# One z pair moved out of the direct stretch, sums of y moved into the merge, and first loads by three queues, in a Mamba/short-conv/SwiGLU block

## The chip, the cores and the metric

The kernel runs on one core of one Trainium2 chip. Its time is the device time of one execution in microseconds (us), the median of several runs; lower is better. A core has five engines that work side by side, each on a queue of its own in the order of the program: PE (TensorE, matrix products; its weight loads are listed as PEld), DVE (VectorE, elementwise), ACT (ScalarE, activations and scaled copies), POOL (GpSimd) and SP (SyncE). Transfers between the chip's memory (HBM) and the on-chip memory (SBUF) are started by an instruction on SP's, ACT's or POOL's queue and then run on 16 DMA engines. An instruction that waits for its data holds up whatever stands behind it in its own queue. PSUM is the small memory of eight banks into which PE writes.

## The reference

One encoder block on x of 1024 rows by 1024 columns, all in float32:

```
h  = rmsnorm(x)
z, xbc, dt, s_b, s_c, s_x, g_a, g_b = split(h @ w_in)
xbc = silu(causal conv of 4 taps(xbc) + bias);  xs, B, C = split(xbc)
y   = chunked state-space scan(xs, softplus(dt + bias), -exp(a_log), B, C) + d_skip * xs
y   = y * silu(z);  y = rmsnorm of y in 4 groups of 512 columns * ssd_norm_w
a   = y @ w_ssd_proj
b   = (s_b * causal conv of 3 taps(s_c * s_x)) @ w_sconv_proj
h1  = x + (sigmoid(g_a) * a + sigmoid(g_b) * b) @ w_o
h2  = h1 + (silu(n @ w_gate) * (n @ w_up)) @ w_down,   n = rmsnorm(h1)
out = rmsnorm(h2) * final_norm_w
```

## The kernel before

Everything is kept transposed: features on the 128 partitions, the 1024 time steps along the row. A tile is 128 features by 1024 steps. A float32 product is made of three matmuls on operands split in a rounded high part and the rest (`split`, lines 68 to 78: ACT writes the high part at line 73 or 76, DVE the low part at line 74 or 77; `mmc`, lines 678 to 681: high by high, low by high, high by low). SBUF is a pool of 47 pages of 512 KB; a new tile takes a page whose former user has ended, and its first writer, often a DMA, waits for that.

The engines' order is that of the program (`manual_schedule`); generators (`side`, `aux`, `scans`) are stepped by hand between the products.

The stages follow each other on PE:

1. **Start.** Eight row blocks `xt` of x are loaded. `rows_sq` squares the first four on ACT and DVE in turn, `rstd_of` makes the root (on ACT, line 101), `rows_scale` scales, PE transposes (line 1543), ACT and DVE copy out with the norm's weight, whose columns `cols` come from small loads by POOL and a transpose (lines 1532 to 1534). `second_half` (line 1592) does the other four and makes the sums T1 to T4 that the seven-product scheme needs, and `put` splits them.
2. **Pairs** (to about 619 us). Products with w_in run for pairs of tiles in a Strassen-like scheme: `Pair` has seven products of 4 k steps for two tiles. Rows in `z_pairs` are tiles 0 to 11 of z.
3. **Direct stretch** (619 to 952.6 us). `direct` (line 974) holds 20 tiles in plain form, 2 halves of 8 k steps each: z tiles 12 to 15, then the 16 gate tiles. Beside it runs the scan: 4 groups by 8 chunks, `part1` and `part2` for each, 65 steps spread by `due` (line 1003) over the direct tiles. When half a group is done, `norm` (line 502) is appended to `norms`: y by z, squares on ACT, the sum of squares by PE, root, transpose `prt`, a copy `rst` on ACT, a write to `rs_d` by POOL and a broadcast load `rbc` from it by POOL, then the scaling at line 543 and writes to `y_g`. After a group's second half, lines 553 to 559 add its four blocks into the forms T1 to T4 of `yt_d` (four sums on DVE, four writes by POOL). `step_norms` (line 563) steps all live norms, the oldest first.
4. **Merge** (from 952.6 us). A `Stream` of chunks, each a loaded piece of both operands (SP), its split (ACT, DVE) and 4 x 2 k steps x 3 = 24 matmuls: 14 chunks of `gv` (short conv branch), 28 of `gy` (scan branch; products 1 and 2 read `y_g`, 6, 5, 7 and 4 read T2, T1, T3 and T4 from `yt_d`), then `go`. Step number `at` emits the loads of chunks up to at + 3, the splits up to at + 1 and the product of chunk at - 1. The last norm of the scan is stepped beside it.
5. **FFN**: `first_half` and `second_half` (lines 1183 and 1191) normalise and transpose h1 and make T1 to T4 (sums on DVE); then 11 units of seven products, and the down product.
6. **Tail**: `fin` (line 1483) for four row blocks: last addition, squares on ACT, `finish` (line 1421: sum of the two halves' squares on DVE, root on ACT, a Newton step on DVE), the two halves scaled by ACT and DVE, one store by SP.

Of the kernel before, what the change touches and what calls it, by code (L numbers as in the profile page):

```python
# [8 lines left out]
F32 = mybir.dt.float32  # L9
# [30 lines left out]
def hybrid_block(ctx: ExitStack, tc: tile.TileContext, x, nmw, w_in, cw, cb, dtb, alog, dsk, snw,  # L40
# [116 lines left out]
    class Slab:  # L157
# [4 lines left out]
        def load(self):  # L162
            if self.st is None:
                self.st = page(self.s + "s", self.shape)
                nc.sync.dma_start(self.st, self.src)
# [62 lines left out]
    warm = cp.tile([P, 1], F32, name="warm")  # L228
    nc.scalar.activation(warm, epst, AF.Sqrt)
    for i in range(4):  # L230
        nc.sync.dma_start(xt[i], x[i * P:(i + 1) * P, :])
# [11 lines left out]
    def more_loads():  # L243
        for i in range(4, NT):
            nc.sync.dma_start(xt[i], x[i * P:(i + 1) * P, :])
# [256 lines left out]
    def norm(g, hf, y0, y1):  # L502
# [38 lines left out]
        for r in range(4):  # L541
            z = ys[r // 2][:, r % 2]
            V.scalar_tensor_tensor(z, z, snc(4 * g + r), rbc, op0=ALU.mult, op1=ALU.mult)
            if r % 2:
                yield
                if hf == 0 or r > 1:
                    nc.gpsimd.dma_start(y_g[g][128 * (r - 1):128 * (r + 1), o].rearrange("(r p) l -> p r l", p=P),
                                      ys[r // 2])
        if hf == 0:
            kept[g] = ys  # L550
            return

        b11, b21 = kept.pop(g)
        b12, b22 = ys
# [5 lines left out]

    def scans():


        def step_norms():
            for n in list(norms):
                if next(n, 0) == 0:
                    norms.remove(n)

        def one(f, j):
            f(j)  # L570
            step_norms()

        want(0, 0)
        want(0, 2)
        prep(0)
        prep(1)
        prep_eb(1)
        yield
        prep2(0)
        for j in range(len(items)):  # L580
            one(part1, j)
            yield
            if j > 0:
                one(part2, j - 1)
                yield
        one(part2, len(items) - 1)
        yield
        while norms:
            step_norms()
            yield  # L590
# [318 lines left out]
    z_pairs = [Pair(i * P, (silu_z(i), silu_z(i + 1))) for i in range(0, 12, 2)]  # L909
# [64 lines left out]
    direct = [(wslab(w_in, i * P), z_raw(i)) for i in range(12, 16)]  # L974
# [188 lines left out]
    def ffn_phase():  # L1163
# [19 lines left out]
        def first_half():  # L1183
            rows0 = h1_rows(0, (2, 3))
            yield
            yield
            yield from fill(rows0, raw0, 0, wcol)
            yield from put("B11", raw0[0])
            yield from put("B21", raw0[1])

        def second_half(rows):
            yield from fill(rows, raw1, 1, wcol)
            t1 = [page("t1", HB) for _ in range(2)]
            for k in range(2):
                V.tensor_add(t1[k], raw1[0][k], raw0[0][k])
            t2 = [page("t2", HB) for _ in range(2)]
            for k in range(2):
                V.scalar_tensor_tensor(t2[k], raw1[1][k], -1.0, t1[k], op0=ALU.mult, op1=ALU.subtract)
            raw0[0].clear()
            every(put("T2", t2))  # L1200
            yield
            every(put("T1", t1))
            yield
            for k in range(2):
                V.tensor_add(raw1[0][k], raw1[1][k], raw1[0][k])
            every(put("T3", raw1[0]))
            yield
            every(put("B22", raw1[1]))
            yield
            for k in range(2):  # L1210
                V.tensor_sub(raw0[1][k], raw0[1][k], t2[k])
            every(put("T4", raw0[1]))
            yield
# [193 lines left out]
        def rstd2_of(ssq, n, s):  # L1407

            shp = list(ssq.shape)
            r = sp.tile(shp, F32, tag="rr", name=nm(s + "r"))  # L1410
            nc.scalar.activation(r, ssq, AF.Sqrt, scale=1.0 / n, bias=epst)
            v = sp.tile(shp, F32, tag="rv", name=nm(s + "v"))
            V.tensor_scalar(v, ssq, 1.0 / n, EPS, op0=ALU.mult, op1=ALU.add)
            V.reciprocal(r, r)
            q = sp.tile(shp, F32, tag="rq", name=nm(s + "q"))
# [5 lines left out]
        def finish(ms):  # L1421
            s = sp.tile([P, len(ms), 1], F32, tag="fss", name=nm("fss"))
            V.tensor_add(s, sq[:, ms[0]:ms[-1] + 1, 0:1], sq[:, ms[0]:ms[-1] + 1, 1:2])
            return rstd2_of(s.rearrange("p a b -> p (a b)"), D, "f")
# [57 lines left out]

        def fin(m):
            t = 4 + m
            r = finish(range(t, t + 1))
            nc.scalar.activation(fo[t][:, 512:1024], h1[t][:, 512:1024], AF.Copy, scale=r)
            out_rows(t, r, 0)
            nc.sync.dma_start(out[t * P:(t + 1) * P, :], fo[t])
# [9 lines left out]
    more_loads()  # L1498
    for p in first[1:]:
        p.y.load()  # L1500
    nc.sync.dma_start(wdt_s, w_in[:, DT0:DT0 + H].rearrange("(k p) f -> p k f", p=P))
    for p in first:
        p.x.load()
    small_loads()
# [23 lines left out]
    a0 = rows_sq(xt[0:4], "x", "avav")  # L1528
    a1 = rows_acc(xt[4:8], "x")
    del xt  # L1530
    pc = bank("pc")
# [60 lines left out]
    def second_half():  # L1592
        t1, t2 = [[page("t1", HB) for _ in range(2)] for _ in range(2)]
        for k in range(KT):
# [9 lines left out]
            if k == 3:  # L1604
# [3 lines left out]
                every(put("T1", t1))  # L1608
            yield
        every(put("T2", t2))  # L1610
# [81 lines left out]
    T.clear()  # L1692
    while ms.at < len(gv.chunks) + len(gy.chunks):
# [3 lines left out]
        ms.step()  # L1697
        pump_scan({1: 2, 2: 2, 4: 3}.get(ms.at, 1 if ms.at < 12 else 2))
        pump(2)
        pump_aux()  # L1700
    ffn_phase()
# [27 lines left out]
```

## Time and profile before

| | us |
|---|---|
| median of 3 runs (1908.9 to 1910.7) | 1909.17 |
| the profiled execution | 1910.68 |
| its span, first to last instruction | 1908.9 |
| PE busy in it | 1879.7 |

The profile is of one execution: it gives each instruction's start and length, the idle time before it, and what ended that idle time (from semaphore events). Views used below: the waits (who waited for whom), the timeline of one engine, the windows (busy time by engine in a stretch), and the DMA view (issues, size, median time to landing). Matmuls are pipelined, so a matmul's listed length (0.39 us) is longer than its distance from the next (about 0.23 us).

### The profile page before, as it was taken

The numbers are of one execution on the slowest core, as the hardware profiler recorded it, in microseconds if no ns is written. First come the engines' busy times: TensorE is split into PE (matmuls) and PEld (weight loads), VectorE is DVE, ScalarE is ACT, GpSimd is POOL, SyncE is SP. The second block draws the span as 40 slices with busy tenths as digits, with TensorE's granted clock in tenths as the row PEclk, the third lists the DMA queues.
The fourth block names the chain that finished last, engine by engine and source line by source line (L and its number), as shares of the span: only waits on it lengthen the run. The fifth ranks groups of instructions, "written<-read, shape, count | busy, mean of one in ns | idle before, by whom it ended". The sixth has DMA issues, their size and how long they took to land.

```text
span 1908.9 us, 24143 instructions
## 1 busy us (share of the span) xinstructions
PE 1879.7 (98%) x8905; PEld 1545.3 (81%) x8905; DVE 1299.4 (68%) x1688; ACT 970.6 (51%) x1541; POOL 169.7 (9%) x196
## 2 busy tenths in 40 slices
PE   7999999999999999999999999999999999999998
PEld 5688888888888888888878888887888888888886
DVE  7667878777785678889878548877444444456465
ACT  5545454444444987877665454464333333345333
POOL 1010111101100000101010000101211121100000
PEclk9999999999999999999999999999999999999999
DMA  5197999978959656778798665917988888867552
GB/s 181 48 275 173 240 230 236 240 187 226 264 149 288 223 194 219 251 250 269 261 321 311 226 208 203 229 80 171 215 193 220 195 193 192 232 257 286 190 196 110
DMA packets 341190, 411.97 MB, mean 216 GB/s; under 512 B 17384, under 2 KB 223936, under 8 KB 341072
## 3 DMA queue, kind: packets, MB, share of 16 engines
q1 hardware_dynamic: 284400, 308.59, 50.0%
q0 software_dynamic: 48608, 72.47, 20.9%
q10 hardware_dynamic: 8064, 29.36, 3.8%
q8 instruction: 70, 1.15, 0.2%
q14 instruction: 48, 0.39, 0.1%
HBM read 320.56 MB, written 143.15 MB: 243 GB/s over the span
## 4 chain that ended last, share of the span: by engine, by line
PE 92%; DVE 4%; ACT 2%; DMA 1%; issue 1%; SPq 0%; ACTq 0%; DVEq 0%
PE pb L679 5%; PE pb L680 5%; PE pb L681 5%; PE gb L679 5%; PE gb L680 5%; PE gb L681 5%; PE fb L681 4%; PE fb L679 4%; PE fb L680 4%; PE pr L81 4%; PE pr L83 4%; PE pr L82 4%; PE gd L679 4%; PE pd L679 4%; PE gd L681 4%; PE gd L680 4%
## 5 line engine op out<-in xcount | busy, mean ns | idle before, releaser
L77 DVE TENSOR_TENSOR wl<-ws,wh 128x1024 fp32r<-128x1024 f32 x77 | 94.0, 1221 | 121.6 <-ACT wh L76 121.6
L679 PE MATMUL gb<-qh,gh 128*128 128x512 f32 x432 | 169.1, 391 | 1.1 <-DVE h L1132 1.1
L680 PE MATMUL gb<-ql,gh 128*128 128x512 f32 x432 | 168.9, 391 | 0.0
L681 PE MATMUL gb<-qh,gl 128*128 128x512 f32 x432 | 168.7, 391 | 0.0
L681 PE MATMUL fb<-th,wl 128*128 128x512 f32 x352 | 137.1, 389 | 0.8 <-DVE wl L77 0.8
L679 PE MATMUL fb<-th,wh 128*128 128x512 f32 x352 | 137.1, 390 | 0.6 <-ACT wh L76 0.6
L680 PE MATMUL fb<-tl,wh 128*128 128x512 f32 x352 | 137.0, 389 | 0.0
L81 PE MATMUL pr<-th,wh 128*128 128x512 f32 x320 | 131.1, 410 | 0.0
L679 PE MATMUL gd<-qh,gh 128*128 128x512 f32 x324 | 126.0, 389 | 0.0
L680 PE MATMUL gd<-ql,gh 128*128 128x512 f32 x324 | 126.0, 389 | 0.0
L681 PE MATMUL gd<-qh,gl 128*128 128x512 f32 x324 | 126.0, 389 | 0.0
L83 PE MATMUL pr<-th,wl 128*128 128x512 f32 x320 | 125.1, 391 | 0.0
L82 PE MATMUL pr<-tl,wh 128*128 128x512 f32 x320 | 124.9, 390 | 0.0
L76 ACT ACTIVATE qh<-cb 128x1024 fp32r<-128x1024 f32 x98 | 99.8, 1018 | 38.0 <-PE gb L680 17.1
L77 DVE TENSOR_TENSOR ql<-cb,qh 128x1024 fp32r<-128x1024 f32 x98 | 115.6, 1180 | 1.6 <-ACT qh L76 1.4
L74 DVE SCALAR_TENSOR_TENSOR gl<-ca,gh 128x1024 fp32r<-128x1024 f32 (+1 forms) x60 | 70.5, 1174 | 49.0 <-ACT gh L73 49.0
L681 PE MATMUL fd<-th,wl 128*128 128x512 f32 x264 | 102.7, 389 | 0.0
L679 PE MATMUL fd<-th,wh 128*128 128x512 f32 x264 | 102.7, 389 | 0.0
L680 PE MATMUL fd<-tl,wh 128*128 128x512 f32 x264 | 102.7, 389 | 0.0
L679 PEld LDWEIGHTS gb<-qh,gh 128*128 128x128 f32 x432 | 81.5, 189 | 18.4 <-DVE h L1132 1.4
L679 PE MATMUL pb<-th,wh 128*128 128x512 f32 x240 | 94.4, 394 | 1.0 <-ACT u L894 1.0
L681 PEld LDWEIGHTS gb<-qh,gl 128*128 128x128 f32 x432 | 81.5, 189 | 17.1
(324 smaller groups left out, 4702.3 us busy)
## 6 DMA issues: line engine op xcount, KB each, us to landing
ws<-in_w_in_dram SPq DMA_DIRECT2D x80, 512.0 KB, 6.3
ws<-in_w_gate_dram SPq DMA_DIRECT2D x77, 256.0 KB, 3.9
ws<-in_w_up_dram SPq DMA_DIRECT2D x77, 256.0 KB, 4.4
ca<-u_d SPq DMA_DIRECT2D x35, 512.0 KB, 5.3
ab<-ac_d SPq DMA_DIRECT2D x32, 512.0 KB, 6.0
xbc_g<-cv ACTq DMA_DIRECT2D x24, 512.0 KB, 7.0
ws<-ws POOLq DMA_DIRECT2D x22, 512.0 KB, 6.4
wd_d<-in_w_down_dram SPq DMA_DIRECT2D x20, 512.0 KB, 10.8
```

The costliest lines, as they stand in the source:

```text
L74: nc.vector.scalar_tensor_tensor(lo, src, -1.0, hi.bitcast(F32), op0=ALU.mult, op1=ALU.subtract)
L76: nc.scalar.activation(hi, src, AF.Copy)
L77: nc.vector.tensor_sub(lo, src, hi.bitcast(F32))
L81: nc.tensor.matmul(o, lh, rh, start=first, stop=False)
L82: nc.tensor.matmul(o, lh, rl, start=False, stop=False)
L83: nc.tensor.matmul(o, ll, rh, start=False, stop=last)
L679: nc.tensor.matmul(o, lh, rh, start=first, stop=False, skip_group_check=True)
L680: nc.tensor.matmul(o, lh, rl, start=False, stop=False, skip_group_check=True)
L681: nc.tensor.matmul(o, ll, rh, start=False, stop=last, skip_group_check=True)
```

## The change

- Tiles 12 and 13 of z go from `direct` to `z_pairs`: 18 direct tiles, seven z pairs.
- For groups 0 to 2, `norm` writes all of y to `y_g` and ends there. Their four sums are made in the merge by `late_sums`, from rows that POOL reads back from `y_g` into four pages `yb` for each group. It is stepped once for each chunk from at = 10, twice from at = 14; the reads of the next group are issued after the group's second sum. Group 3 is summed in its norm as before.
- `step_norms` steps the newest norm first.
- First loads: x by SP and ACT in turn, the rest of x by ACT between the squares, the weight slabs after the first one, wdt and the x slabs by POOL.
- `second_half` of the start splits T2 one slot earlier.
- FFN: ACT scales one row block of the first half instead of two; the sum for T3 is made by an accumulating DMA of POOL instead of DVE.
- Tail: the known half of the squares' sum goes into the root's bias, made ahead; the last block is stored in two halves by ACT and SP.

```diff
-        def load(self):
+        def load(self, eng=None):
             if self.st is None:
                 self.st = page(self.s + "s", self.shape)
-                nc.sync.dma_start(self.st, self.src)
+                (eng or nc.sync).dma_start(self.st, self.src)
...
+    for i in range(4):
+        (nc.scalar if i % 2 else nc.sync).dma_start(xt[i], x[i * P:(i + 1) * P, :])
     nc.scalar.activation(warm, epst, AF.Sqrt)
-    for i in range(4):
-        nc.sync.dma_start(xt[i], x[i * P:(i + 1) * P, :])
...
-    def more_loads():
-        for i in range(4, NT):
-            nc.sync.dma_start(xt[i], x[i * P:(i + 1) * P, :])
+    def more_loads(i):
+        for i in (i, i + 1):
+            nc.scalar.dma_start(xt[i], x[i * P:(i + 1) * P, :])
...
-                if hf == 0 or r > 1:
+                if hf == 0 or r > 1 or g < G - 1:
                     nc.gpsimd.dma_start(y_g[g][128 * (r - 1):128 * (r + 1), o].rearrange("(r p) l -> p r l", p=P),
                                       ys[r // 2])
+        if g < G - 1:
+            return
         if hf == 0:
             kept[g] = ys
             return
-
-        b11, b21 = kept.pop(g)
-        b12, b22 = ys
+        yield from y_sums(g, kept.pop(g), ys)
+
+    def y_sums(g, y_0, y_1):
+
+        b11, b21 = y_0
+        b12, b22 = y_1
         t1, t2 = page("s1", HB), page("s2", HB)
         for t, a, b, f in ((t1, b11, b12, "T1"), (t2, t1, b22, "T2"), (b12, b12, b22, "T3"), (b21, b21, t2, "T4")):
             V.tensor_add(t, a, b)
             nc.gpsimd.dma_start(yt_d[f][256 * g:256 * g + 256, :].rearrange("(k p) f -> p k f", p=P), t)
             yield
 
+    def late_sums():
+
+        def back(g):
+            r = []
+            for hf in range(2):
+                r.append([page("yb", HB) for _ in range(2)])
+                for i in range(2):
+                    nc.gpsimd.dma_start(r[hf][i], y_g[g][256 * i:256 * i + 256, hf * 512:hf * 512 + 512]
+                                        .rearrange("(r p) l -> p r l", p=P))
+            return r
+
+        nxt = back(0)
+        yield
+        for g in range(G - 1):
+            now, nxt = nxt, None
+            for i, _ in enumerate(y_sums(g, *now)):
+                if i == 1 and g + 1 < G - 1:
+                    nxt = back(g + 1)
+                yield
+            del now
...
-            for n in list(norms):
+            for n in norms[::-1]:
...
-    z_pairs = [Pair(i * P, (silu_z(i), silu_z(i + 1))) for i in range(0, 12, 2)]
+    z_pairs = [Pair(i * P, (silu_z(i), silu_z(i + 1))) for i in range(0, 14, 2)]
...
-    direct = [(wslab(w_in, i * P), z_raw(i)) for i in range(12, 16)]
+    direct = [(wslab(w_in, i * P), z_raw(i)) for i in range(14, 16)]
...
-            rows0 = h1_rows(0, (2, 3))
+            rows0 = h1_rows(0, (3,))
...
             raw0[0].clear()
+            for k in range(2):
+                nc.gpsimd.dma_start(raw1[0][k], raw1[1][k], accum_op=ALU.add)
             every(put("T2", t2))
             yield
             every(put("T1", t1))
             yield
-            for k in range(2):
-                V.tensor_add(raw1[0][k], raw1[1][k], raw1[0][k])
             every(put("T3", raw1[0]))
...
+        known = sp.tile([P, 4], F32, tag="rv", name=nm("fk"))
+        V.tensor_scalar(known.unsqueeze(2), sq[:, 4:8, 1:2], 1.0 / D, EPS, op0=ALU.mult, op1=ALU.add)
+
         def fin(m):
             t = 4 + m
-            r = finish(range(t, t + 1))
+            r = rstd2_of(sq[:, t, 0:1], known[:, m:m + 1])
             nc.scalar.activation(fo[t][:, 512:1024], h1[t][:, 512:1024], AF.Copy, scale=r)
             out_rows(t, r, 0)
-            nc.sync.dma_start(out[t * P:(t + 1) * P, :], fo[t])
+            if m < 3:
+                nc.sync.dma_start(out[t * P:(t + 1) * P, :], fo[t])
+            else:
+                nc.scalar.dma_start(out[t * P:(t + 1) * P, 512:1024], fo[t][:, 512:1024])
+                nc.sync.dma_start(out[t * P:(t + 1) * P, 0:512], fo[t][:, 0:512])
...
-    a0 = rows_sq(xt[0:4], "x", "avav")
+    a0 = rows_acc(xt[0:4], "x")
+    rows_sq_on("a", a0, "x")
+    more_loads(4)
+    rows_sq_on("v", a0, "x")
+    rows_sq_on("a", a0, "x")
+    more_loads(6)
+    first[1].y.load(nc.gpsimd)
+    nc.gpsimd.dma_start(wdt_s, w_in[:, DT0:DT0 + H].rearrange("(k p) f -> p k f", p=P))
+    first[2].y.load(nc.gpsimd)
+    rows_sq_on("v", a0, "x")
     a1 = rows_acc(xt[4:8], "x")
     del xt
+    for p in first:
+        p.x.load(nc.gpsimd)
+    small_loads()
...
-            yield
-        every(put("T2", t2))
+            if k == 7:
+                every(put("T2", t2))
+            yield
         yield
...
+    late = late_sums()
     while ms.at < len(gv.chunks) + len(gy.chunks):
...
         ms.step()
+        for _ in range(0 if ms.at < 10 else 1 if ms.at < 14 else 2):
+            next(late, None)
         pump_scan({1: 2, 2: 2, 4: 3}.get(ms.at, 1 if ms.at < 12 else 2))
```

`rstd2_of` takes the bias in place of the constant, so that the root is of ssq / 1024 + known.

More of the change, by code (lines that the diff above doesn't have):

```diff
@@ L1405, in squares, with rstd2_of @@
             nc.scalar.activation(fo[t][:, no], h1[t][:, no], AF.Square, accum_out=sq[:, t, j:j + 1])
-        def rstd2_of(ssq, n, s):
+        def rstd2_of(ssq, b):
             shp = list(ssq.shape)
[L1410 to L1413, printed above, removed]
+            r = sp.tile(shp, F32, tag="rr", name=nm("fr"))
+            nc.scalar.activation(r, ssq, AF.Sqrt, scale=1.0 / D, bias=b)
+            v = sp.tile(shp, F32, tag="fv", name=nm("fv"))
+            V.tensor_scalar(v, ssq, 1.0 / D, b, op0=ALU.mult, op1=ALU.add)
             V.reciprocal(r, r)
-            q = sp.tile(shp, F32, tag="rq", name=nm(s + "q"))
+            q = sp.tile(shp, F32, tag="rq", name=nm("fq"))
             V.tensor_mul(q, r, r)
@@ L1423, in finish @@
             V.tensor_add(s, sq[:, ms[0]:ms[-1] + 1, 0:1], sq[:, ms[0]:ms[-1] + 1, 1:2])
-            return rstd2_of(s.rearrange("p a b -> p (a b)"), D, "f")
+            return rstd2_of(s.rearrange("p a b -> p (a b)"), epst)
         def out_rows(t, r, n):
@@ L1497, in hybrid_block @@
     first[0].y.load()
[L1498 to L1504, printed above, removed]
     loaded[0] = NF
@@ L1700, in hybrid_block @@
         pump_aux()
+    every(late)
     ffn_phase()
```

## The prediction

> **What bounds the kernel now.** The page's span and busy table come first; then the waits of PE (engine, line, what it waited for: total, times, longest), of which one row stands here, the others at their places.
>
> ```profile
> span 1908.9 us, 24143 instructions
> PE 1879.7 (98%) x8905; PEld 1545.3 (81%) x8905; DVE 1299.4 (68%) x1688; ACT 970.6 (51%) x1541; POOL 169.7 (9%) x196
> PE prt L532 <- DVE gr L107: 2.1, 1, 2.1
> ```
>
> PE is the bound: only 1908.9 - 1879.7 = 29.2 us are not its work, most of them before its first matmul and behind its last. So the time can fall in three ways: fewer matmuls, fewer of the few waits inside, a shorter head or tail. It rises where another engine makes PE wait anew. I go through the change by that.
>
> **Two tiles of z as a pair.** A direct tile costs 2 halves x 8 k x 3 = 48 matmuls, a pair of tiles 7 products x 4 k x 3 = 84. Two tiles thus go from 96 to 84 matmuls. What one costs is read from a stage where PE never waits (windows: length, busy and count by engine PE, PEld, DVE, ACT, POOL, then clock, DMA share, GB/s):
>
> ```profile
> 1400.00:1600.00 200.00, 200.00 (x884) 165.67 (x883) 89.18 (x107) 66.92 (x91) 37.36 (x32) 1.00 0.83 200
> 800.00:900.00 100.00, 100.00 (x627) 82.57 (x626) 88.82 (x148) 79.61 (x189) 8.96 (x14) 1.00 0.81 264
> L81 PE MATMUL pr<-th,wh x320: 389/389/499, 619.0 to 951.9; 128*128 128x512 f32 x160
> ```
>
> 200 / 884 = 0.226 us, and 12 x 0.226 = **-2.7 us**. The price to check is the cover: the scan's 65 steps now lie beside 18 direct tiles, not 20. The direct stretch (619 to 952.6, about 334 us) loses 96 x 0.226 = 21.7 us, so the scan runs 334 / 312 = 1.07 times as dense. In 800 to 900 DVE was 89% busy and PE waited for nothing. Sums of y that leave are 4 of about 1.2 us per 83 us group, 5%; (0.89 - 0.05) x 1.07 = 0.90. Equal, so I cost it at nothing; the upper end is one stall like `prt`'s, 2.1 us. POOL's three extra writes of y (0.7 us each) lie in idle time.
>
> **The wait at `prt`.** The rows of ACT, POOL and DVE before it (start, length, engine, line, operation, count, idle time before and what ended it):
>
> ```profile
> 958.31 0.27 ACT L534 ACTIVATE rst<-prt 4x128 f32<-4x128 f32 x1 [0.64 <-PE prt L532]
> 964.32 0.72 POOL L558 DMA_DIRECT2D yt_d<-y  x1 [2.69 <-DVE y L557]
> 965.03 0.53 POOL L536 DMA_DIRECT2D rs_d<-rst  x1
> 972.20 0.57 POOL L538 DMA_DIRECT2D rbc<-rs_d  x1 [6.64 <-PE gd L681]
> 979.12 2.74 DVE L543 SCALAR_TENSOR_TENSOR y<-y,cols,rbc 128x512 f32<-128x512 f32 x4 [2.89 <-DMA rbc<-rs_d]
> ```
>
> The row sums were ready at 958.6, but POOL wrote them at 965.0: in its queue they stood behind `yt_d` writes of group 2, which waited for DVE's sums. DVE then stood 2.9 us before `rbc`, with the last norm's root queued behind it, and PE waited for that. The change takes group 2's sums from here (rs_d leaves some 6 us earlier) and steps the newest norm first. 6 us is more than 2.9, so the wait goes: **-2.1 us** (at the least half of it, if `rbc` waits for its page as long as now).
>
> **FFN.** Rows of ACT, DVE and PE:
>
> ```profile
> 1248.35 1.42 DVE L137 TENSOR_SCALAR hn<-h,nr 128x1024 f32<-128x1024 f32 x2
> 1248.41 2.19 ACT L135 ACTIVATE hn<-h,nr 128x1024 f32<-128x1024 f32 x2 [1.10 <-DVE nr L107]
> 1251.58 1.23 DVE L74 SCALAR_TENSOR_TENSOR gl<-mc,gh 128x1024 fp32r<-128x1024 f32 x1 [1.81 <-ACT gh L73]
> 1254.60 0.50 PE L679 MATMUL gb<-qh,gh 128*128 128x512 f32 x1 [1.13 <-DVE h L1132]
> 1284.37 2.35 DVE L1195 TENSOR_TENSOR t<-br,br 128x1024 f32<-128x1024 f32 x2
> 1298.79 2.00 ACT L76 ACTIVATE th<-br 128x1024 fp32r<-128x1024 f32 x2
> ws<-ws POOLq DMA_DIRECT2D x22, 512.0 KB, 6.4
> ```
>
> With one row scaled on ACT instead of two, ACT reaches `gh` 1.1 us sooner; DVE's third scale (half of 1.42) fits into its 1.81 us of idling. The eviction that PE waits for comes 1.1 us earlier: **-1.1 us** (0.8 to 1.1). The T3 sum by an accumulating DMA saves DVE 2 x 1.2 us, but PE waits for nothing of it: nothing gained. It is issued when DVE has made t1, at 1286.7; POOL has nothing before it then, so 1286.7 + 2 x 0.7 (an issue of POOL, as above) + 6.4 = 1294.5, ahead of ACT's split at 1298.8. Cover 4.3 us, cost nothing; with twice the landing it is 2.1 us late, and ACT and DVE have 1 us of room before PE's use: some 1 us.
>
> **T2 put one slot earlier (start).**
>
> ```profile
> 53.19 1.41 DVE L1602 SCALAR_TENSOR_TENSOR t<-pt,cols,t 128x512 f32<-128x512 f32 x2 [1.34 <-ACT br L1600]
> 56.37 1.99 ACT L76 ACTIVATE th<-t 128x1024 fp32r<-128x1024 f32 x2
> 57.46 0.49 PE L679 MATMUL pb<-th,wk 128*128 128x512 f32 x1 [0.45 <-ACT th L76]
> 58.72 0.50 PE L680 MATMUL pb<-tl,wk 128*128 128x512 f32 x1 [0.77 <-DVE tl L77]
> ```
>
> t2 is ready at 54.6 and split from 56.4, because the slot's own work comes between. Placed first, the split starts near 53.7 and 54.7; PE's 0.45 + 0.77 = 1.22 us shrink. The pushed-back `wk` split ends at about 57.6 and takes part of it back: **-0.8 us** (0.3 to 1.2).
>
> **First loads by three queues.** Rows of ACT, DVE and PE, and one of ACT's DMA issues from later:
>
> ```profile
> 8.41 1.06 ACT L117 ACTIVATE xn<-x 128x1024 f32<-128x1024 f32 x1 [3.16 <-DMA x<-in_x_dram]
> 9.86 1.23 DVE L115 SCALAR_TENSOR_TENSOR xn<-x 128x1024 f32<-128x1024 f32 x1 [3.13 <-DMA x<-in_x_dram]
> 10.30 0.36 PE L1533 MATMUL pc<-ident,c 80*128 80x80 f32 x1 [1.88 <-DMA c<-in_sconv_w_dram]
> 10.70 0.32 ACT L1534 ACTIVATE cols<-pc 128x176 f32<-128x176 f32 x1 [1.14 <-PE pc L1533]
> 11.41 0.20 ACT L101 ACTIVATE nr<-nv 128x4 f32<-128x4 f32 x1 [0.39 <-DVE nv L99]
> 936.54 0.33 ACTq L658 DMA_DIRECT2D ga_a<-gt  x1
> ```
>
> x may land 1 to 1.5 us sooner. But what is late next is at hand: `cols` stands ahead of the root in ACT's queue and waits for POOL's load of sconv_w, which lands at 10.3. The root can come forward by its own idle time only, 0.39 us. Against it, POOL's small loads now share the engines with two other queues instead of one, and no row shows that; if sconv_w lands at 12 the root is 2 us late less its 0.39. So -0.4 to +1.7; near the row, at 11, I take **+0.3 us**. ACT's six issues of 0.33 us lie in its idle 3.16 and 1.14; the slabs y1, y2 and wdts on POOL are used from 20 us on.
>
> The Trainium skill, page "DMA: Bandwidth & Descriptors", section "Issuing engines are not separate DMA queues", says that all issuers share the same 16 engines and only issue time is saved. By it x lands no sooner here, so that the best end of -0.4 falls away, and the split of the last store below brings nothing: the sum would be 0.3 us higher.
>
> **Tail.**
>
> ```profile
> 1903.25 0.16 DVE L1423 TENSOR_TENSOR fss<-sqf 128x1 f32<-128x1 f32 x1 [0.79 <-ACT fo L1405]
> 1904.55 0.72 ACT L1486 ACTIVATE fo<-h,fr 128x512 f32<-128x512 f32 x1 [0.81 <-DVE fr L1418]
> ```
>
> The sum before the root goes from the last tile's chain: 0.2 us. ACT's half of the last store leaves when ACT is done instead of behind DVE: some 0.3 us. **-0.5 us** (0.2 to 0.7).
>
> **Sums of three groups in the merge.** Here it can go wrong. DVE's rows from the 12th chunk on (c0 is the merge's first; pairs of L74 and L77 are a chunk's split, the row at 1031.48 follows c14's), a window, and from the DMA view the size and the time to landing:
>
> ```profile
> 1016.60 1.22 DVE L74 SCALAR_TENSOR_TENSOR gl<-ca,gh 128x1024 fp32r<-128x1024 f32 x1
> 1031.48 1.22 DVE L557 TENSOR_TENSOR y<-y,s 128x1024 f32<-128x1024 f32 x1
> 1044.09 1.22 DVE L77 TENSOR_TENSOR gl<-ca,gh 128x1024 fp32r<-128x1024 f32 x1
> 1045.23 1.22 DVE L77 TENSOR_TENSOR ql<-cb,qh 128x1024 fp32r<-128x1024 f32 x1
> 1057.49 1.23 DVE L77 TENSOR_TENSOR gl<-ca,gh 128x1024 fp32r<-128x1024 f32 x1 [11.05 <-ACT gh L76]
> 1077.67 0.69 DVE L1052 TENSOR_TENSOR mc<-mc,gd 128x512 f32<-128x512 f32 x1 [0.67 <-PE gd L681]
> 1030.00:1040.00 10.00, 10.00 (x46) 8.29 (x45) 10.00 (x12) 4.86 (x5) 0.71 (x1) 1.00 1.02 383
> z<-z_g SPq DMA_DIRECT2D x16, 512.0 KB, 5.0
> vt_d<-v_g POOLq DMA_DIRECT2D x4, 512.0 KB, 12.4
> SPq L1104 <- DMA yt_d<-y: 8.5, 1, 8.5
> ```
>
> The row at 1077.67 evicts what c21 made last, so c21 ends there; at 24 x 0.227 = 5.44 us a chunk c14 starts at 1034.1, c16 at 1045.0, c18 at 1055.9. DVE works without a gap from c12's split (1016.6) to the end of c19's (1046.4), then idles 11 us. A row of 1.22 us starts 1.14 after the one before it, so a split takes 2.27: c14's ended at 1031.5, and back from 1046.4 c17's at 1041.8, c16's at 1039.6. The change puts 12 sums of 1.14 us in there, one per chunk from c10 on, two from c13 on. Adding them in queue order, c14's split ends 2 sums later, 1033.8 (in time by 0.3), c16's 5 sums later, 1045.3: PE waits **0.4**. The reads: group 0's go out a chunk ahead of use in a queue that is idle, group 1's about 15 us ahead. Group 2's are issued behind T2 of group 1 (DVE ends it at 1046.5) and its write, 0.7 us each; between lie only T3, c17's split and T4, 4.5 us of DVE. T1 needs the third read: issued at +2.2, and landing 5.5 later (nearest the 5.0 of z's reads, of the same shape), it is there at +7.7. DVE waits 3.2 us; c18's split, queued behind, ends at 1046.5 + 7.7 + 1.14 + 2.27 = 1057.6 against 1056.3: PE waits 1.3, say **1.5**. Behind that DVE gains 0.9 us a chunk, and its 11 idle us swallow the rest. Together **+1.9 us**; the ends are 0.4 (the read there at +6.4) and some 12 (below).
>
> Sum: -2.7 - 2.1 - 1.1 - 0.8 - 0.5 + 0.3 + 1.9 = **-5.0 us**. The profiled execution took 1910.7 (its span and 1.8 around it) and would take 1905.7; the median shown is 1909.17, 1.5 below it, so the forecast is **1904.2 us**.
>
> **The rivals.**
> 1. The third read is there at +6.4 or sooner, and c18 isn't late. For it: four reads stream together, and 5.0 counted from the first one's issue is +5.7. Against it: POOL's queue shares a busy DMA. Time: 1904.2 - 1.5 = 1902.7. The Trainium skill, same page, section "Anatomy of one DMA — SWDGE (gpsimd) path", gives 2.0 us plus bytes at 436 GB/s; for the three reads that is, as an estimate, 5.6 us, so +6.3 and this rival's time; no row shows reads of POOL in a row.
> 2. A merge stall of 5 us. The window 1030 to 1040 has DMA at 1.02 of its engines' time, and 12 reads and 12 writes come in. With the read at +11 instead of +7.7 the stall grows by 3.3: 1907.5, no measurable change.
> 3. The constants land 2 us later than the 10.3 of now: 1904.2 - 0.3 + 1.7 = 1905.6, no measurable change.
> 4. Slower. Group 2's reads need pages; if these are those that group 0's last write (T4 at 1042, landing 0.7 + 7.7 later, 1050.4) sets free, POOL stands until then, as SP did for 8.5 us on `yt_d<-y`. With 2.2 and the slowest POOL row, 12.4, the read lands at 1065.0, c18 is split at 1068.4, PE stands 12.1 us: 1904.2 - 1.5 + 12.1 = 1914.8. It decides from a stall of 10.3 us on (1913.0). Against it: pages are freed every chunk by PE, and four to six chunks of loads stand ready.
>
> **How the numbers follow.** Forecast (1903 to 1905.3) 0.46, rival 1 (or a gain beyond it) 0.16, rival 2 0.22, rival 3 0.08, rival 4 0.08. 0.2% is 3.8 us, about what a measurement of this kernel can tell: faster (under 1905.35) 0.46 + 0.16 = 0.62, same 0.30, slower 0.08. The range reaches from 1901.0 (rival 1 and the start's best end, and somewhat more) to 1908.5 (rival 2 and a part of the start's loss); rival 4 and the far ends of both, 2 in 10, are left out.
>
> **What would show it.** `pr` has 288 matmuls per line, `pb` and `pd` more; no wait at `prt`, `gb <- h L1132` or T2's split; the root of the first rows at 11.0 to 11.7; a wait of DVE for `yb` before T1 of group 2, and waits of PE at c16 and c18 alone. Wrong would be: PE waits in the direct stretch, chunk loads late behind POOL's traffic, or SP held by pages of `yb`.

## The result, and the profile after

| | us |
|---|---|
| before, median of 19 runs beside it (1907.5 to 1910.7) | 1908.9 |
| after, median of 19 runs (1911.2 to 1914.0) | 1911.86 |
| ratio, with its 95% interval | 1.0015 [1.0008, 1.0022] |
| the profiled execution after; its span | 1912.67; 1910.3 |

The changed kernel is 0.15% slower. That is under the 0.2% that the prediction took as the least that counts, and the interval (0.08% to 0.22%) leaves out that it is faster. The forecast was 1904.2, in 1901.0 to 1908.5.

The page of the changed kernel, then rows of PE's waits (total, times, longest):

```profile
span 1910.3 us, 24163 instructions
PE 1877.0 (98%) x8893; PEld 1542.2 (81%) x8893; DVE 1303.7 (68%) x1694; ACT 968.4 (51%) x1541; POOL 188.2 (10%) x219
```

```profile
PE gd L707 <- DVE ql L77: 7.0, 1, 7.0
PE pc L1573 <- DMA c<-in_sconv_w_dram: 1.6, 1, 1.6
...
PE poff L476 <- ACT st L483: 0.6, 1, 0.6
```

PE has the 12 matmuls less, and 2.7 us less work. The waits at `prt` and at `gb <- h` are gone. In their place stands one of 7.0 us at `gd`, in chunk c18. DVE's rows around it, from its timeline (start, length, engine, line, operation, count, idle time before and what ended it):

```profile
1037.90 1.22 DVE L563 TENSOR_TENSOR s<-s,yb 128x1024 f32<-128x1024 f32 x1
...
1042.44 1.22 DVE L563 TENSOR_TENSOR yb<-yb,s 128x1024 f32<-128x1024 f32 x1
1052.67 1.22 DVE L563 TENSOR_TENSOR s<-yb,yb 128x1024 f32<-128x1024 f32 x1 [9.01 <-DMA yb<-y_g]
1053.81 1.22 DVE L77 TENSOR_TENSOR gl<-ca,gh 128x1024 fp32r<-128x1024 f32 x1
1054.94 1.22 DVE L77 TENSOR_TENSOR ql<-cb,qh 128x1024 fp32r<-128x1024 f32 x1
```

The first sum of group 2 (1052.67) waits 9.0 us for its rows, and c18's split stands behind it in DVE's queue. It is the place that the prediction named; it gave the wait 3.2 us. PE's timeline there:

```profile
1048.82 0.39 PE L706 MATMUL gd<-qh,gh 128*128 128x512 f32 x1
1056.22 0.79 PE L707 MATMUL gd<-ql,gh 128*128 128x512 f32 x1 [7.01 <-DVE ql L77]
1056.81 0.63 PE L708 MATMUL gd<-qh,gl 128*128 128x512 f32 x1
1057.23 0.63 PE L706 MATMUL gd<-qh,gh 128*128 128x512 f32 x1
...
1059.80 0.56 PE L706 MATMUL gd<-qh,gh 128*128 128x512 f32 x1
1060.19 0.39 PE L707 MATMUL gd<-ql,gh 128*128 128x512 f32 x1
```

The wait isn't the whole loss. From 1056.22 to 1060.19 nine matmuls take 3.97 us, 0.44 each instead of 0.227: 1.9 us more. The windows of these two stretches (length, busy and count by engine PE, PEld, DVE, ACT, POOL, then clock, DMA share, GB/s) show what goes with it: the granted clock is 0.67 in the second one. The DMA engines are full in both.

```profile
1040.00:1050.00 10.00, 9.21 (x41) 7.30 (x39) 3.66 (x4) 5.01 (x7) 4.38 (x7) 1.00 1.03 416
1050.00:1060.00 10.00, 3.78 (x9) 3.01 (x10) 7.33 (x7) 3.17 (x3) 2.15 (x3) 0.67 1.03 414
```

Who asked for transfers at that time is read from the timelines of POOL and of SP's queue:

```profile
1036.00 0.72 POOL L564 DMA_DIRECT2D yt_d<-s  x1 [0.42 <-DVE s L563]
1039.42 0.71 POOL L564 DMA_DIRECT2D yt_d<-s  x1 [2.69 <-DVE s L563]
1040.12 2.84 POOL L574 DMA_DIRECT2D yb<-y_g  x4
1042.94 0.73 POOL L564 DMA_DIRECT2D yt_d<-yb  x1
```

```profile
1025.40 0.37 SPq L761 DMA_DIRECT2D ca<-in_w_ssd_proj_dram  x1
1039.22 0.36 SPq L1131 DMA_DIRECT2D cb<-y_g  x1
1039.67 0.46 SPq L761 DMA_DIRECT2D ca<-in_w_ssd_proj_dram  x1
1040.23 0.49 SPq L1131 DMA_DIRECT2D cb<-y_g  x1
1040.82 0.47 SPq L761 DMA_DIRECT2D ca<-in_w_ssd_proj_dram  x1
1041.41 0.47 SPq L1131 DMA_DIRECT2D cb<-y_g  x1
```

```profile
SPq L1131 <- DMA yt_d<-y: 13.4, 1, 13.4
```

SP stood 13.4 us (last row, from the waits of SP's queue) for a page that a write of sums still held, and then sent five chunk loads within 2.2 us, the same in which POOL sent the four reads of group 2. Twelve transfers of 512 KB between 1036.0 and 1043.7 are 6.3 MB; at 416 GB/s that is 15 us. What landing took, from the DMA view of three windows, 986 to 996, 1019 to 1029 and 1039 to 1053 us (what moved in the window, then some of the transfers issued in it: count, size, median us to landing):

```profile
DMA packets 1411, 3.62 MB, mean 362 GB/s; under 512 B 122, under 2 KB 122, under 8 KB 1410
...
yb<-y_g POOLq DMA_DIRECT2D x4, 512.0 KB, 6.4
...
cb<-y_g SPq DMA_DIRECT2D x1, 512.0 KB, 6.8
...
DMA packets 1535, 3.55 MB, mean 355 GB/s; under 512 B 109, under 2 KB 109, under 8 KB 1534
...
yb<-y_g POOLq DMA_DIRECT2D x4, 512.0 KB, 11.0
...
cb<-y_g SPq DMA_DIRECT2D x1, 512.0 KB, 16.1
...
yb<-y_g POOLq DMA_DIRECT2D x4, 512.0 KB, 10.5
cb<-y_g SPq DMA_DIRECT2D x3, 512.0 KB, 14.5
```

The `yb` rows are the reads of group 0 (from 989.0), group 1 (1020.7) and group 2 (1040.1). The engines' busy share was 1.03, 1.00 and 1.03 in the three windows, so the share doesn't tell them apart. What differs is how much is asked for: in the first window 6 transfers of 512 KB are issued in 10 us, in the second 11. SP's loads beside the reads took longer too, 14.5 us instead of 6.8, so it is not POOL's queue alone that was slow. By the stages of both traces, the part from the first `gb` to the first `fb` grew from 314.8 to 319.4 us (949.26 to 1268.64), although two waits of PE left it; all that lies before it became 3.3 us shorter.

### The profile page after: what moved, and what is told of

It reads as the page before. It is cut to its first block, busy times and chain, and to the rows that moved or that the text cites. A ratio compares the mean times of both kernels' runs of the same rounds, so it can differ in the third digit from the quotient of the medians.

```text
span 1910.3 us, 24163 instructions
## 1 busy us (share of the span) xinstructions
PE 1877.0 (98%) x8893; PEld 1542.2 (81%) x8893; DVE 1303.7 (68%) x1694; ACT 968.4 (51%) x1541; POOL 188.2 (10%) x219
## 4 chain that ended last, share of the span: by engine, by line
PE 90%; DVE 4%; ACT 3%; DMA 2%; issue 1%; POOL 0%; ACTq 0%; SPq 0%; DVEq 0%; POOLq 0%
PE pb L706 6%; PE pb L707 5%; PE pb L708 5%; PE gb L706 4%; PE gb L707 4%; PE gb L708 4%; PE fb L708 4%; PE fb L706 4%; PE fb L707 4%; PE pd L706 4%; PE pd L707 4%; PE pd L708 4%; PE gd L707 4%; PE gd L708 4%; PE gd L706 4%; PE pr L81 3%
## 5 line engine op out<-in xcount | busy, mean ns | idle before, releaser
L81 PE MATMUL pr<-th,wh 128*128 128x512 f32 x288 | 118.7, 412 | 0.0
L83 PE MATMUL pr<-th,wl 128*128 128x512 f32 x288 | 112.6, 391 | 0.0
L82 PE MATMUL pr<-tl,wh 128*128 128x512 f32 x288 | 112.4, 390 | 0.0
L891 ACT ACTIVATE wh<-ws 128x1024 fp32r<-128x1024 f32 x62 | 65.7, 1059 | 64.7 <-DVE ws L878 59.7
L707 PE MATMUL pb<-tl,wh 128*128 128x512 f32 x248 | 96.8, 390 | 1.5 <-DVE tl L77 1.5
## 6 DMA issues: line engine op xcount, KB each, us to landing
wd_d<-in_w_down_dram SPq DMA_DIRECT2D x20, 512.0 KB, 10.5
```

Source lines behind the costliest of these rows:

```text
L81: nc.tensor.matmul(o, lh, rh, start=first, stop=False)
L82: nc.tensor.matmul(o, lh, rl, start=False, stop=False)
L83: nc.tensor.matmul(o, ll, rh, start=False, stop=last)
L707: nc.tensor.matmul(o, lh, rl, start=False, stop=False, skip_group_check=True)
L891: nc.scalar.activation(t[0], self.source(what), AF.Copy)
```

## The experiments

All medians are beside runs of the kernel before on the same chip; "merge" is the time from the first `gb` to the first `fb` in the profile.

| kernel | median us | ratio to before, 95% | merge us |
|---|---|---|---|
| before (the profile shown; another one) | | | 314.8; 313.0 |
| after | 1911.86 | 1.0015 [1.0008, 1.0022] | 319.4 |
| sums_in_norm | 1903.24 | 0.9969 [0.9956, 0.9981] | 310.7 |
| same_rows | 1902.68 | 0.9967 [0.9956, 0.9979] | 310.2 |
| reads_sooner | 1904.86 | 0.9977 [0.9968, 0.9985] | 312.2 |
| one_a_chunk | 1907.22 | 0.9989 [0.9980, 0.9998] | 315.6 |
| reads_by_need | 1910.41 | 1.0008 [0.9999, 1.0017] | 317.6 |
| two_ahead_one_store | 1902.97 | 0.9968 [0.9955, 0.9980] | 311.0 |
| fewer_writes | 1902.71 | 0.9966 [0.9953, 0.9979] | 310.2 |
| group2_kept | 1903.34 | 0.9963 [0.9950, 0.9977] | 310.7 |
| late_alone | 1917.50 | 1.0043 [1.0031, 1.0056] | 321.7 |
| z_alone | 1908.41 | 0.9994 [0.9985, 1.0003] | 315.1 |
| old_start | 1903.22 | 0.9968 [0.9956, 0.9981] | 311.1 |
| two_ahead_old_start | 1903.52 | 0.9970 [0.9960, 0.9981] | 311.3 |

The theory at the start: the loss is one stall at c18, because group 2's rows are asked for right behind T2 of group 1. The rivals: DVE's twelve sums are too many for the merge; the transfers are too many; or the loss is in another part.

**sums_in_norm.** The late sums undone, all else kept.

```diff
-                if hf == 0 or r > 1 or g < G - 1:
+                if hf == 0 or r > 1:
...
-        if g < G - 1:
-            return
...
-        for _ in range(0 if ms.at < 10 else 1 if ms.at < 14 else 2):
-            next(late, None)
```

> The changed kernel with the sums of groups 0 to 2 made in their norms again; all the rest of the change stays. Theory (group 2's rows are read back too late): the wait of PE at gd <- ql (7.0 us) goes, with the slow clock behind it, 7.7 us together: 1911.9 - 7.7 = 1904.2 us; since group 2's sums stand in POOL's queue ahead of rs_d again, up to 2.1 us of waiting at prt may come back: 1904.2 to 1906.3. Rival (the time went into another part: the denser scan, the start): the gd wait goes, but others take its place, 1909 or more.

1903.24: the loss is in the late sums, and without them the rest of the change gains 0.31%. PE's wait at `prt` is 0.5 us here, though group 2's sums stand in POOL's queue again: what is left to take it is stepping the newest norm first, which no run has alone.

**same_rows.** Twelve sums and twelve writes, but only group 0's rows are read. The kernel leaves out eight reads, so it doesn't compute the block.

```diff
-                if i == 1 and g + 1 < G - 1:
-                    nxt = back(g + 1)
...
+            yield from y_sums(g, *nxt)
...
+            if g < G - 1 and f in ("T3", "T4"):
+                t = page("yb", HB)
```

> The changed kernel with the rows of groups 1 and 2 not read back: their sums are made from the four pages of group 0, and T3 and T4 written to pages of their own. It leaves out 8 reads of 512 KB; the sums on DVE and the writes of yt_d are as many as before. Theory (reads too late): nothing waits for yb, PE's gd wait goes, 1904.2 us. Rival (DVE's load): the gd wait stays at 4 us or more, 1908 to 1911.9. Rival (too many transfers): between the two, with chunk loads still late.

```profile
1040.00:1050.00 10.00, 10.00 (x46) 8.29 (x45) 10.00 (x10) 3.55 (x6) 3.36 (x5) 1.00 1.02 396
1050.00:1060.00 10.00, 10.00 (x46) 8.29 (x45) 6.51 (x6) 3.70 (x4) 0.71 (x1) 1.00 1.04 409
```

The same windows as above, of this kernel: PE is never idle, with as many sums on DVE. DVE's load is not the cause. The merge of this kernel, 310.2 us, is the measure for one without the stall: the stall cost 319.4 - 310.2 = 9.2 us.

**reads_sooner.** The reads are issued ahead of the group's first sum.

```diff
-            now, nxt = nxt, None
+            now, nxt = nxt, back(g + 1) if g + 1 < G - 1 else None
```

> The changed kernel with the next group's reads issued ahead of a group's first sum instead of behind its second. Theory (reads too late): group 2's reads are issued when T4 of group 0 is made, at about 1034.6 instead of 1039.1, so with the same 13.6 us they are there at 1048.2 instead of 1052.7: DVE's wait shrinks from 9.0 to 4.5, PE's from 7.0 to 2.5 us, 1907.4 us. Rivals (DVE's load, or the number of transfers): no change, 1911.9.

The reads went out at 1034.56, DVE took their rows at 1046.29 and waited 3.6 us; PE waited 1.7. The mechanism is as expected, the gain larger (7.0 us for 4.5): behind the wait of 1.7 us the clock stayed at 1.00, so the slow stretch went too.

**one_a_chunk.** One late step for each chunk.

```diff
-        for _ in range(0 if ms.at < 10 else 1 if ms.at < 14 else 2):
+        for _ in range(0 if ms.at < 10 else 1):
```

> The changed kernel with one late step for each chunk to the end (none doubled from at = 14). Same sums, same reads, same writes. Theory (reads too late): the rows of group 2 are asked for three chunks (over 16 us) ahead of their first sum, more than the 13.6 us that they took; DVE's wait for yb is under 1 us, PE's gd wait goes, 1904 to 1905 us. Rival (DVE's twelve sums are too many for the merge): the sums only come later, PE waits some 4 us or more in all, 1908 or more. Rival (the transfers are too many): loads of chunks or of T2 come late instead, SP waits on yt_d for longer and PE at a chunk from c22 on, 1906 to 1910.

Two rows of DVE's waits:

```profile
DVE gl L77 <- DMA yt_d<-s: 7.2, 1, 7.2
...
DVE s L563 <- DMA yb<-y_g: 2.3, 1, 2.3
```

The wait for `yb` shrank to 2.3 us, but T2 of group 2 was now written only at 1061.5. Until that write had landed, at 1068.4, SP stood 8.2 us before a chunk's load and DVE 7.2 us before a split; PE waited 3.6 us in two places up to 1084.8, again with a slow stretch (clock 0.83). My estimate was wrong: it counted the reads only. The rival of the late loads holds in this kernel: the sums can be too late as well as their rows.

**reads_by_need.** The four reads in the order of use.

```diff
+            for hf, i in ((0, 0), (1, 0), (1, 1), (0, 1)):
```

> The changed kernel with the four reads of a group in the order in which the sums want them (the first sum needs the first two instead of the first and the third). Theory that reads of one queue land one after another: the second lands 2 to 3 us ahead of the third, DVE waits 6 to 7 us instead of 9.0, 1909 to 1910. Rival (the queue's reads share the engines and land nearly together): DVE waits 8 to 9 us, 1911 or more.

DVE waits 7.3 instead of 9.0 us, PE 5.3 instead of 7.0. The time, 1910.41, lies between the two forecasts. The rows of the first sum were there 10.9 us behind the first issue instead of 12.6: one place earlier in the queue is worth 1.7 us, of which 0.7 is the issue itself, and not 2 to 3.

**two_ahead_one_store.** The reads two groups ahead, and one store for the last block.

```diff
+        rows.append(back(1))
...
+                if g == 0 and i == 2:
+                    rows.append(back(2))
...
-            else:
-                nc.scalar.dma_start(out[t * P:(t + 1) * P, 512:1024], fo[t][:, 512:1024])
-                nc.sync.dma_start(out[t * P:(t + 1) * P, 0:512], fo[t][:, 0:512])
```

> The changed kernel with the reads of group 1 issued ahead of the first sum of group 0 and those of group 2 behind T3 of group 0 (two groups ahead), and the last row block stored by SP in one piece. Theory (reads too late, nothing else in the merge): the rows of group 2 are there before DVE wants them, DVE waits for yb under 1 us, the merge takes as long as with the same rows (310.2 us from the first gb to the first fb); the rival, that the full DMA only moves the lateness to a chunk's loads, gives a PE wait of 2 us or more at a chunk from c16 on. One store: from the start of the last scale of fo to the end 4.8 us became 4.35 as in the kernel before, if the two halves were what cost; 4.8 if not. Time 1902 to 1903; with the rival 1904 or more.

DVE waits for `yb` nowhere, PE 0.5 us at one chunk, 1902.97. The reads of group 2, issued at 1027.9, still took 10.2 us; only nothing waits for them now. The end was misjudged: it is 4.8 us from the last scale, with one store as with two.

**fewer_writes.** Groups 0 and 1 summed and written in their norms, and summed again in the merge without being written.

```diff
-        if g < G - 1:
+        if g == G - 2:
...
+            if write:
...
+            for i, _ in enumerate(y_sums(g, *now, write=g == G - 2)):
```

> The changed kernel with the sums of groups 0 and 1 made and written in their norms as before, and made again in the merge without being written: the reads of all three groups and the twelve sums stay where they are, eight writes of 512 KB fewer lie beside them. Theory (the rows of group 2 are late because all 16 DMA engines are full, 1.03 at 416 GB/s): with 1.5 to 3 MB less asked for before and beside them they land 4 to 7 us sooner than the 12.6 us from the first issue, DVE waits for yb 2 to 5 us instead of 9.0, the merge from the first gb to the first fb takes 311 to 315 us instead of 319.4. Rival (reads of POOL's queue take this long whatever else runs): they land after 12 us or more, DVE waits 8 us or more, 318 us or more.

No wait, 1902.71, yet not for the reason expected. Without the writes of groups 0 and 1 POOL waits for DVE less often, so the reads of group 2 went out at 1030.60, ten us sooner; and they took 10.2 us, with the DMA engines at 1.04 and 413 GB/s, and five of SP's loads issued beside them. So this run doesn't isolate the load. What the rows of all runs give is that reads issued between 986 and 1004 land in 6.4 to 7.4 us (medians of four), the four issued here from 1015.7 in 8.8, and those issued from 1019 on in 9.6 to 11.3.

For SP's own loads there are runs with less beside them. Those of `ss_d`, issued from 1039 to 1053 us, in the changed kernel, in same_rows and in sums_in_norm:

```profile
ca<-ss_d SPq DMA_DIRECT2D x1, 512.0 KB, 18.0
...
ca<-ss_d SPq DMA_DIRECT2D x3, 512.0 KB, 11.7
...
ca<-ss_d SPq DMA_DIRECT2D x2, 512.0 KB, 3.9
```

In these 14 us the three kernels issue 16, 14 and 5 transfers of 512 KB. The count is not the whole of it (this kernel issues 10, and its loads of `ss_d` take 14.8 us), but the same load is slow where much is asked for. For the reads of group 2 themselves it stays a reading: no run issued them at that moment with little beside them.

**late_alone and z_alone.** The kernel before with one part of the change each: the late sums as in the change, or

```diff
+    z_pairs = [Pair(i * P, (silu_z(i), silu_z(i + 1))) for i in range(0, 14, 2)]
...
+    direct = [(wslab(w_in, i * P), z_raw(i)) for i in range(14, 16)]
```

> The kernel before with the late sums alone (groups 0 to 2 in the merge from rows read back, the steps of the change). Theory: the wait at prt goes, the gd wait at c18 comes; from the stages of the runs so far (314.8 us from the first gb to the first fb before, 319.4 after the change, of which the FFN part is 1.1) 314.8 to 320.5, so 5.7 us slower than before: 1914.5. Rival (the late sums hurt only because the denser scan and the moved start put them at a bad moment): under 1911.

> The kernel before with tiles 12 and 13 of z as a pair, nothing else. Theory (12 matmuls of 0.226 us, the denser scan costs nothing): 2.7 us faster, 1906.1, and no PE wait in the direct stretch over 1 us. Rival (DVE's cover is used up): a PE wait of 1 to 2 us at a scan or direct tile, 1907 to 1909.

The late sums alone cost 8.5 us: DVE waits 9.8 us for `yb`, PE 7.8, and the clock is low in two windows (0.74, 0.75). More than expected, the same place. The wait at `prt` is gone here too, with the oldest norm still stepped first: moving the sums takes it alone.

The pair alone measured -0.6 us, with an interval from -2.9 to +0.6: the medians don't decide. The times do, because they lie in two groups, as those of the kernel before do (see before_again). The pair has 4 of 11 near 1907.0 and 7 near 1908.7, the kernel before beside it 10 of 15 near 1908.6 and 5 near 1910.6 (means): group by group the pair gains 1.6 to 1.8 us, and more of its runs fell into the longer group. Its stages agree: the direct stretch is 312.9 instead of 333.6 us, 20.7 less where 96 matmuls make 21.7, and `poff` waits 0.6 us for ACT; the pairs, counted from 77 us on, grow by 19.1 (84 x 0.226 = 19.0). So the pair gains 1.6 us, and the denser scan costs 1.0.

**old_start and two_ahead_old_start.** The first loads as before, on sums_in_norm and on two_ahead_one_store:

```diff
-        (nc.scalar if i % 2 else nc.sync).dma_start(xt[i], x[i * P:(i + 1) * P, :])
+        nc.sync.dma_start(xt[i], x[i * P:(i + 1) * P, :])
...
-    first[1].y.load(nc.gpsimd)
+    for p in first[1:]:
+        p.y.load()
```

> The changed kernel with the sums in the norm (1903.2 us) and the first loads as in the kernel before (x, slabs and wdt by SP). Theory from the profiles (first pb at 17.8 to 18.9 us in five profiles with the new loads, 19.3 before): the new loads are worth 0.4 to 1.5 us, 1904.2 (1903.6 to 1904.7). Rival (as predicted, constants later: a loss of 0.3): 1902.9.

> Reads two groups ahead and one last store, with the first loads of the kernel before. Theory: the first loads by three queues make the stage of the start 0.4 us shorter and the end 0.45 us later (4.8 us instead of 4.35 from the last scale to the end, in every kernel with them, whatever the store), so this is within 0.5 us of 1903.0, and its end is 4.35. Rival (the end is later for another reason): 4.8 again.

1903.22 beside 1903.24, and 1903.52 beside 1902.97: the three queues bring nothing that these runs can tell. The start shows no difference either: the first `pb` comes at 17.8 to 19.6 us in nine profiles with them and at 17.7 to 19.8 in six without. The end did move as the theory had it: in every profile with the three queues the end, from the last scale of `fo` on, takes 4.8 us; in all six with the loads of before it takes 4.3 to 4.4, with one store and with two. Why the first loads show at the end stays open.

**before_again.** The kernel before, for a second profile.

> The kernel before once more, for its profile: its times lie in two clusters, near 1908.5 (granted clock 0.999) and near 1910.5 (0.998), and the profile shown is of the slower one. Theory: the two differ by the stretch of slow matmuls behind the wait at prt (8 at 0.43 us instead of 0.23, 1.6 us); where the wait is shorter it is not there. A profile of the faster cluster would show the prt wait without slow matmuls behind it, from the first gb to the first fb 313 us instead of 314.8; one of the slower cluster 314.8 again. Rival: the clusters differ in the start.

```profile
983.39 0.27 PE L532 MATMUL prt<-ident,gr 128*4 128x128 f32 x1 [1.92 <-DVE gr L107]
983.42 0.49 PE L679 MATMUL gb<-qh,gh 128*128 128x512 f32 x1
...
984.21 0.40 PE L679 MATMUL gb<-qh,gh 128*128 128x512 f32 x1
```

In the profile shown before, PE waited 2.12 us at `prt`, and the matmuls from 984.31 to 987.30 are 0.43 us apart. Here it waited 1.92, the matmuls after it come at 0.23 us, and the merge is 313.0 instead of 314.8 us: as expected. The times of the kernel before lie in two groups 2 us apart (of 22 beside the first experiments 14 from 1908.1 to 1909.4, 8 from 1910.0 to 1911.3), and the two profiles differ in the merge by this stretch. The profile of z_alone, of its longer group, has the stretch too. That the stretch makes the groups is thus likely, from three profiles, and not shown.

**group2_kept.** Only group 2 summed late, from the pages in which its y still stands.

```diff
+        if g == G - 2:
+            kept[g] = kept[g], ys
...
+        yield from y_sums(G - 2, *kept.pop(G - 2))
```

> The changed kernel with one store at the end, the sums of groups 0 and 1 in their norms again, and those of group 2 alone in the merge, one for each chunk from at = 10, made from the pages in which its y still stands: no row is read back. Theory (of the late sums only the moment and the reads cost; moving group 2's sums out of the way of rs_d is what pays): no wait for yb, none at prt, none at gd; from the first gb to the first fb 310.2 us as with the same rows, 1902 to 1903. Rival (moving sums into the merge costs by itself, or four pages held for longer make the chunks' loads late): a PE wait of 1 us or more from c10 on, or SP held by pages, 1904 or more.

1903.34, no wait for rows and none at `prt`, but PE waits 0.7 us at a chunk. Summing in the merge costs next to nothing; it brings next to nothing either. Six kernels without the stall (sums_in_norm, two_ahead_one_store, fewer_writes, group2_kept, old_start, two_ahead_old_start) lie within 0.8 us, and these runs can't rank them; all six beat both kernels by 0.3% or more. The simplest is sums_in_norm: the change without its late sums.

## Why the prediction was wrong

By its terms, against the profiled execution of before; what the profiles show, and which part of it a run bears out:

| term | predicted | measured |
|---|---|---|
| z pair | -2.7 | -1.6 (stages; z_alone) |
| T2 one slot earlier | -0.8 | -0.7, and -0.5 of unknown cause later |
| wait at `prt` | -2.1 | -3.7 (2.1 and the slow stretch) |
| FFN | -1.1 | -1.1 |
| start | +0.3 | -0.25 in this profile; nothing to be seen by old_start |
| tail | -0.5 | -0.3 to the last scale, +0.45 behind it |
| late sums | +1.9 | +9.2 |

These sum to +1.5 us; the spans differ by 1.4. The stages of the two profiles say the same: the first `pb` 0.4 sooner, the pairs 18.0 longer, the direct stretch 20.9 shorter, the merge 4.6 longer, the rest 0.1 longer.

**The late sums** are the step that failed, and in it one number: "issued at +2.2, and landing 5.5 later (nearest the 5.0 of z's reads, of the same shape), it is there at +7.7". The place, the queue behind it and the chunk were right. The rows were there at +13.6: DVE ended T2 at 1039.1 and took them at 1052.7. The third read went out at +2.4 (1041.5), as forecast, so its landing took 11.1 us and not 5.5. The 0.4 us at c16 didn't come: PE's waits list none there. I chose the row by shape and not by time. In the trace of before, the DMA view of just the window in which the reads were to fall has the right one:

```profile
ca<-in_w_ssd_proj_dram SPq DMA_DIRECT2D x4, 512.0 KB, 9.0
cb<-y_g SPq DMA_DIRECT2D x4, 512.0 KB, 10.5
```

That is 1020 to 1045, without the reads; the 5.0 of z was a median over the whole program. With 10.5 the rows are there at +12.7, DVE waits 8.2 us and c18's split ends at 1046.5 + 12.7 + 1.14 + 2.27 = 1062.6, 6.3 us late: beside the 7.0 measured. Rival 2 had the mechanism (busy engines) with +11 and a price of 5 us; rival 4 was as near in price, 12.1, but by pages for `yb`, and POOL waited for none ahead of group 2's reads (before group 0's it stood 4.7 us). Pages did play a part, elsewhere: SP stood 13.4 us for one, and its five loads then went out beside the reads. No run shows what that alone cost.

The rule of the Trainium skill, page "DMA: Bandwidth & Descriptors", section "Anatomy of one DMA — SWDGE (gpsimd) path", gave 5.6 us for the three reads, and the trace disagrees: 12.6 us from the first issue to the sum. The estimate counts these three reads alone; in the trace twelve transfers of this size went out within 7.7 us.

**What followed a stall** was not priced at all: 1.6 to 1.9 us of slow matmuls, which stand in the loss (7.0 became 8.9 of the 9.2) and in the gain (`prt`, 2.1 became 3.7). The profiled execution of before had this stretch; by its time, the median run probably did not.

**The z pair** was right in its count; the cover that I cost at nothing took 1.0 us back, inside the upper end of 2.1 that I gave. I had reckoned with DVE's share; the wait that came is for ACT (`poff`).

**T2** came out as forecast: both waits (1.22 us) vanished, the `wk` split pushed back costs 0.23 us (at 57.48, wait for DVE), and a wait for DVE at 75.8 us grew from 0.27 to 0.76, which the forecast lacked; from 55 to 77 us that is 0.7 us less. Two waits of 0.25 us in the pairs also went, in every kernel with T2 earlier and in none without; why is open. **FFN** was right: the wait at `h` is gone, and the accumulating DMAs, issued at 1287.4 and 1288.5, were done before ACT's split at 1300.0, which waits for nothing. **Start**: sconv_w landed at 9.9 instead of 10.3 and not later, but profiles of kernels with one and the same start differ by more than that. **Tail**: the last scale comes 0.3 us sooner after the first `fb`, but the two scales of `fo` end together (1906.21 and 1906.24), so a second store had nothing to gain. The rule of the Trainium skill, same page, "Issuing engines are not separate DMA queues", that only issue time is saved by more queues, agrees with both: old_start and the store of one or two pieces make no difference that the runs can tell.

The forecast gave a merge stall near 1.5 us a chance of about a half and one of 5 us or more 0.30; the second was the case.

## What to carry to other kernels

Take a transfer's landing time from rows of the same stretch of time, not of the same shape: here 9 to 10.5 us stood in the window where the new reads would go, and 5.0 in the list of the whole program. Ask for data that is read back well ahead of its use, ahead of whatever an in-order queue would put before it: asked for two groups ahead it cost nothing here, asked for 4.5 us of DVE's work ahead it cost 9 us. And try the parts of a change alone: four parts of this one were worth 0.3% together, and one took it all back.

## What was not expected of the hardware

A wait of PE in the merge has a price beyond its length once it is long enough. Behind waits of 1.7 us (reads_sooner) and 1.9 us (before_again) the matmuls came at 0.23 us at once, and the granted clock was 1.00. Behind waits of 2.1 us (before), 2.4 (z_alone), 2.8 (one_a_chunk), 5.3 (reads_by_need), 7.0 (after) and 7.8 (late_alone) there follow nine to twelve slow matmuls, most of them 0.43 us apart: 1.6 to 2.4 us are lost, and the clock of the 10 us window is 0.66 to 0.83. Behind the waits of 2.1 and 2.4 us the first four matmuls still came at 0.23. In these eight traces the border lies between 1.92 and 2.12 us; no run places it more closely or shows what sets it. The kernel before waits just there, and its times fall into two groups, 2 us apart.
